# First expert layer: weights loaded as whole rows of 128 channels, the sums of the contraction kept open in six banks of PSUM

## The chip, the cores and the metric

The kernel runs as one program on one core of one Trainium2 chip. The metric is device microseconds (us) from the start of the program to its end. Three runs of the kernel before gave 3406.78, 3413.11 and 3400.99 us; their median is 3406.78 us.

Five engines work side by side, each on its own list of instructions: TensorE (PE; its loading of weights is shown apart, as PEld), VectorE (DVE), ScalarE (ACT), GpSimd (POOL) and SyncE (SP). SP issues nearly all loads of weights from HBM; 16 DMA engines carry them out. PSUM is the memory into which TensorE writes; it has eight banks of 512 fp32 per partition.

## The reference, cut to what matters

Two models are applied to 512 tokens of 1024 channels, all in fp32. The change touches one part of the first model: its mixture of eight experts, two for each token.

```python
def swiglu(h, w1, w3, w2):
    return (jax.nn.silu(h @ w1) * (h @ w3)) @ w2

def moe_swiglu(h, router_w, router_b, w1, w3, w2):
    logits = (h @ router_w).astype(jnp.float32) + router_b.astype(jnp.float32)
    top_logit, top_idx = lax.top_k(logits, TOP_K)
    top_p = jax.nn.softmax(top_logit, axis=-1)
    ...
    for e in range(N_EXPERTS):
        y = y + gates[..., e:e + 1] * swiglu(h, w1[e], w3[e], w2[e])
    return y
```

For each expert w1 and w3 are 1024 x 1408 and w2 is 1408 x 1024: 17.3 MB of fp32 from HBM for one expert.

## The kernel before, in words

`experts()` computes the layer. The tokens of each expert are counted on the chip; a tree of branches (`choose`) picks a body by the count: one unit is 64 tokens, and there are bodies for 1, 2, 2.25, 2.5, 3 and 4 units. In the profiled execution nine bodies run, in this order: expert 0 with 2 units; experts 1 and 2 with 144 and 160 tokens; expert 3 with 4 units, and the rest of its tokens in a body of 144; experts 4 and 5 with 1 unit; expert 6 with 144 tokens; expert 7 with 1 unit. They stand in the trace from about 1690 to 2385 us. Since each body is code of its own behind a branch, every engine takes branches between two bodies.

There are three kinds of body.

- **Whole** (2.25 and 2.5 units, `whole_weights`): the weight is the stationary operand, 128 x 128 at a time, and 144 or 160 tokens move. The sums stand with channels on the partitions, so the result has to be transposed (L648) before `row_out` (L564, on DVE) scales it.
- **Pieces** (2, 3 and 4 units, in `body`): tokens are stationary, the weight's columns move. For fp32 precision each loaded weight is split into a high and a low part (`split_into`: ACT L77, then DVE L80), and each product is three matmuls (`mm3`, L86, L89, L90).
- **Narrow** (1 unit): high and low parts of 64 tokens lie side by side, so a product with w1 or w3 takes two matmuls (L548 with the weight's high part, L549 with its low part); the product with w2 (`narrow_out`) uses the unsplit weight (L662).

In all three, w1 and w3 are taken in four chunks of their 1408 columns (`widths`: 384, 384, 384, 256). For a chunk, w1 and then w3 are loaded, each in two loads of 512 rows (`w_in`: 128 partitions x 4 row blocks x 384 columns, 768 KB, so pieces of 1536 contiguous bytes; 1024 bytes in the last chunk). The contraction of 1024 is summed at once for one chunk, in one PSUM tile ("up", four buffers), which is evacuated before the next chunk. w2 is taken in four quarters of 256 columns (`w_out`, two loads each, pieces of 1024 bytes); a narrow body takes it in two halves of 512 (pieces of 2048 bytes, L662). That is 24 loads for a body.

A load goes into one of two `raw` buffers of the body's parity (L495) or, three of five, one of three `wraw` buffers (L61), so five are in flight. SP waits at a load until the work on the buffer's last content is done. `nxt()` (the transposes of the next expert's tokens) stands ahead of the last chunk. Expert 7's narrow body adds its results to the output at once (`LastRows`, `take`, L1143 and L1147).

Of the kernel before, what the change touches and what calls it, by code (L numbers as in the profile page):

```python
# [10 lines left out]
F32 = mybir.dt.float32  # L11
# [9 lines left out]
KB = 8  # L21
# [10 lines left out]
class K:  # L32
# [37 lines left out]
    def split_into(self, parts, raw, step=None, eng=None, later=False):  # L70
        nc = self.nc
        hi, lo = parts
        n = raw.shape[1]
        step = step or n
        for i in range(0, n, step):
            c = slice(i, i + step)
# [388 lines left out]
def experts(k, ctx, tag, E, NF, xrows, yrows, dst, src, cnt, w1, w3, w2, variants, most, least=0, sums=None):  # L465
# [10 lines left out]
    n = -(-NFB // 3)  # L476
    widths = [128 * (NFB // n + (i < NFB % n)) for i in range(n)]
    WD = max(widths)
    FH = -(-NFB // 2)
# [19 lines left out]
    def parts(src, shape):  # L499
# [4 lines left out]
        return k.split_into(out, raw, 1 if i == 0 else None)  # L504
# [52 lines left out]
    def w_out(e, c, get):  # L557
        return [get(w2[e][f0 * 128:min(f0 + FH, NFB) * 128, c].rearrange("(fb p) n -> p fb n", p=128),
                    [128, min(FH, NFB - f0), c.stop - c.start]) for f0 in range(0, NFB, FH)]
# [29 lines left out]
    class LastRows:  # L589


        def __init__(self):
            self.now, self.left = {}, None

        def __call__(self, i, c):
            name, bufs = ("silu", 3) if i else (f"gu{c.start // 256 % 2}", 1)
            self.now[i] = hp.tile([128, WD], F32, name=name, bufs=bufs)[:, :256]
            return self.now[i]

        def done(self, q, c, sizes):  # L600
# [3 lines left out]
            self.left = lambda: sums.take(q, c, ys, lambda: pg.tile([128, 2, 256], F32, name="up", bufs=4))  # L604
# [6 lines left out]
    def whole_weights(e, b0, N, rx, nxt):  # L611
# [3 lines left out]
        c0 = 0  # L615
        for ci, n in enumerate(widths):
            f0, nf = c0 // 128, n // 128
            ps = []
            for w in (w1, w3):
                ws = w_in(w, e, c0, n, load)  # L620
                p = pg.tile([128, WD // 128, N], F32, name="up", bufs=4)[:, :nf]
                for f in range(nf):
                    for kb in range(KB):
                        nc.tensor.matmul(p[:, f], lhsT=ws[kb // 4][:, kb % 4, f * 128:(f + 1) * 128], rhs=xf[:, kb, 0:N],  # L624
                                         start=kb == 0, stop=kb == KB - 1)
                ps.append(p)
            h = hid[:, f0:f0 + nf]
            nc.scalar.activation(h, ps[0], AF.Silu)
            nc.vector.tensor_tensor(out=h, in0=h, in1=ps[1], op=OP.mult)  # L629
            c0 += n  # L630
            if ci == len(widths) - 2:
                nxt()
        sizes = [min(128, N - i) for i in range(0, N, 128)]
        ys = results(e, b0, rx)
        for q in range(4):
# [16 lines left out]
    def narrow_out(e, h, ys, share):  # L652

        for m in range(2):
            ps = pg.tile([128, 256], F32, name="yo")
            for f0 in range(0, NFB, 3):
                n = min(3, NFB - f0)
                w = load(w2[e][f0 * 128:(f0 + n) * 128, m * 512:m * 512 + 512].rearrange("(fb p) n -> p fb n", p=128),
                         [128, n, 512])
                for f in range(n):  # L660
                    for j in range(2):
                        nc.tensor.matmul(ps[j * S:j * S + S], lhsT=h[:, f0 + f], rhs=w[:, f, j * 256:j * 256 + 256],  # L662
                                         start=f0 + f == 0, stop=f0 + f == NFB - 1)
            for j in range(2):
                q = 2 * m + j
                c = slice(q * 256, q * 256 + 256)
                row_out(ys(0, c)[0:S], ps[j * S:j * S + S], c, share, j == 0)
                ys.done(q, c, [S])

    def body(e, b0, units, rx, nxt):  # L670
# [13 lines left out]
        c0 = 0  # L684
        for ci, n in enumerate(widths):
            acts = []
            for i, w in enumerate((w1, w3)):
                ws = w_in(w, e, c0, n, parts)
                for (b, half), x, h in zip(pieces, xs, hs):
                    ps = pg.tile([128, WD], F32, name="up", bufs=4)[:, :n]  # L690
                    for kb in range(KB):
                        product(ps, x[:, kb], [m[:, kb % 4] for m in ws[kb // 4]], half, kb == 0, kb == KB - 1)
                    f0, nf = c0 // 128, n // 128
                    if half:
                        g = hp.tile([128, WD], F32, name=f"gu{i}", bufs=1)[:, :n]
                        if i == 0:
                            nc.scalar.activation(g, ps, AF.Copy)
                            acts.append(g)
                            continue
                        nc.vector.tensor_copy(out=g, in_=ps)  # L700
                        pt = [pg.tile([128, nf, S], F32, name="tp") for _ in range(2)]
                        for q, t in enumerate((acts.pop(0), g)):
                            for f in range(nf):
                                nc.tensor.matmul(pt[q][:, f], lhsT=t[:, f * 128:(f + 1) * 128], rhs=two, start=True,
                                                 stop=True)
                        if units == 1:
                            a = h[:, f0:f0 + nf]
                        else:
                            a = hp.tile([128, WD // 128, S], F32, name="silu", bufs=3)[:, :nf]
                        nc.scalar.activation(a, pt[0], AF.Silu)  # L710
                        nc.vector.tensor_tensor(out=a, in0=a, in1=pt[1], op=OP.mult)
                        if units == 1:
                            continue
                    else:
                        if i == 0:
                            s = hp.tile([128, WD], F32, name="silu", bufs=3)[:, :n]
                            nc.scalar.activation(s, ps, AF.Silu)
                            acts.append(s)
                            continue
                        s = acts.pop(0)  # L720
                        nc.vector.tensor_tensor(out=s, in0=s, in1=ps, op=OP.mult)
# [6 lines left out]
            c0 += n  # L728
            if ci == len(widths) - 2:
                nxt()  # L730
        ys = results(e, b0, rx)
        if units == 1:
            narrow_out(e, hs[0], ys, sums and rx[3][:, 0:1])
            return
# [1905 lines left out]
```

## Time and profile before

| | |
|---|---|
| median of three runs | 3406.78 us (3400.99 to 3413.11) |
| the profiled execution: time, span of its records | 3420.45 us, 3418.6 us |
| mean granted clock of TensorE | 0.895 |
| instructions in the trace | 46334 |
| PE, PEld, DVE, ACT, POOL busy, share of the span | 87%, 70%, 51%, 38%, 16% |
| the nine bodies of the expert layer | about 1690 to 2385 us of the span |

The mean shares hide that the stages have different limits. In the rows further down a stretch of time is a line: the busy time of each engine in it with the number of instructions, the TensorE clock that was granted (1.00 is full speed), and the busy share of the DMA engines. A stage whose PE is busy all the time is TensorE's; one in which PE waits and the DMA share is near 1 is the loads'.

### The profile page before, as it was taken

How to read it: one execution, taken by the hardware profiler on the slowest of the kernel's cores; microseconds unless marked ns; L12 is line 12 of the kernel's file. 1: busy time of each engine (PE TensorE's matmuls, PEld its weight loads, DVE VectorE, ACT ScalarE, POOL GpSimd, SP SyncE). 2: the span in 40 equal slices, each digit the busy share in tenths (PEclk: the TensorE clock that was granted, in tenths of full speed). 3: DMA queues.
4: the chain of work that ended last, by engine and by line, in shares of the span. 5: the costliest groups of instructions: out<-in, count | busy, mean ns of one | idle time of the engine just before them, and what ended most of it. 6: DMA issues, size and time to landing. Idle time of an engine off the chain costs nothing. (4 is left out here: it accounts for less than half of the span.)

```text
span 3418.6 us, 46334 instructions
## 1 busy us (share of the span) xinstructions
PE 2960.8 (87%) x18016; PEld 2386.8 (70%) x18016; DVE 1753.9 (51%) x2902; ACT 1294.8 (38%) x2158; POOL 546.1 (16%) x701
## 2 busy tenths in 40 slices
PE   7989988899978499988678798787899969999996
PEld 3566977778767377867678798686676657666663
DVE  2544447775676755446340141604535547656565
ACT  2354433444433321123341241513353535555453
POOL 0011033333242300001400000202210021000001
PEclk8987978998979699999599899998999979999998
DMA  5455533332454455534487657988320149999995
GB/s 194 150 176 183 161 92 106 89 98 74 115 154 131 138 173 182 157 117 130 151 252 219 214 180 227 334 268 278 86 76 13 74 142 412 387 367 375 366 352 195
DMA packets 401120, 648.58 MB, mean 190 GB/s; under 512 B 94174, under 2 KB 300856, under 8 KB 375191
## 3 DMA queue, kind: packets, MB, share of 16 engines
q1 hardware_dynamic: 343290, 529.04, 46.2%
q10 hardware_dynamic: 40558, 56.91, 5.5%
q0 software_dynamic: 16944, 58.55, 5.1%
q8 instruction: 171, 2.80, 0.4%
q14 instruction: 157, 1.29, 0.1%
HBM read 584.81 MB, written 64.33 MB: 190 GB/s over the span
## 5 line engine op out<-in xcount | busy, mean ns | idle before, releaser
L80 DVE TENSOR_TENSOR wlo<-wraw,whi 128x1024 fp32r<-128x1024 f32 (+4 forms) x230 | 378.1, 1652 | 189.7 <-ACT whi L77 188.9
L77 ACT ACTIVATE whi<-wraw 128x1024 fp32r<-128x1024 f32 (+4 forms) x238 | 316.4, 1341 | 410.5 <-PE up L89 202.6
L80 DVE TENSOR_TENSOR wlo<-raw,whi 128x2048 fp32r<-128x2048 f32 (+3 forms) x102 | 205.8, 2020 | 72.0 <-ACT whi L77 71.8
L897 PE MATMUL up<-wlo,xx 128*128 128x512 f32 x512 | 225.0, 440 | 9.4 <-DVE wlo L80 8.9
L897 PE MATMUL up<-whi,xx 128*128 128x512 f32 x512 | 221.0, 432 | 9.9 <-ACT whi L77 8.5
L77 ACT ACTIVATE whi<-raw 128x2048 fp32r<-128x2048 f32 (+4 forms) x114 | 181.5, 1602 | 78.7 <-DMA raw<-in_rk_w_o_dram 25.4
L897 PEld LDWEIGHTS up<-wlo,xx 128*128 128x128 f32 x512 | 104.9, 205 | 78.7 <-issue 28.4
L90 PE MATMUL up<-hhi,wlo 128*128 128x512 f32 x352 | 142.4, 405 | 5.5 <-DVE wlo L80 5.4
L86 PE MATMUL up<-hhi,whi 128*128 128x512 f32 x352 | 142.0, 404 | 4.2 <-DVE hhi L212 4.1
L911 PEld LDWEIGHTS tu<-two,gu 128*128 128x128 f32 x512 | 124.5, 326 | 29.9 <-DVE gu L903 16.5
L89 PE MATMUL up<-hlo,whi 128*128 128x512 f32 x352 | 141.4, 402 | 0.0
L911 PE MATMUL tu<-two,gu 128*128 128x64 f32 x512 | 126.9, 391 | 12.6 <-DVE gu L903 10.5
L2062 POOL TENSOR_TENSOR tb<-Nb,Xb 128x60 f32<-128x60 f32 (+36 forms) x186 | 82.7, 444 | 315.8 <-DMA Nb<-ldram 302.0
L897 PEld LDWEIGHTS up<-whi,xx 128*128 128x128 f32 x512 | 105.8, 207 | 35.3 <-ACT whi L77 14.9
L2023 PE MATMUL pre<-AR,BKm 128*128 128x128 f32 (+1 forms) x768 | 120.5, 308 | 11.3 <-ACT BKm L2020 11.1
L927 PE MATMUL yo<-w2raw,hid 128*64 128x512 f32 x512 | 126.5, 617 | 0.9 <-DVE hid L914 0.9
L624 PE MATMUL up<-xf,raw 128*128 128x144 f32 (+1 forms) x640 | 92.5, 302 | 38.9 <-issue 37.8
L629 DVE TENSOR_TENSOR hs<-hs,up 128x432 f32<-128x432 f32 (+3 forms) x16 | 9.2, 578 | 218.6 <-PE up L624 218.6
L2023 PEld LDWEIGHTS pre<-AR,BKm 128*128 128x128 f32 x768 | 107.1, 216 | 14.8 <-ACT BKm L2020 11.6
L624 PEld LDWEIGHTS up<-xf,raw 128*128 128x128 f32 x640 | 88.4, 201 | 40.1 <-issue 38.8
L2168 DVE SCALAR_TENSOR_TENSOR S<-chain,wc,Sw 64x64 f32<-64x64 f32 x320 | 90.3, 282 | 45.7 <-ACT Y L2158 37.1
L2025 DVE TENSOR_TENSOR G<-pre,mask 128x512 f32<-128x512 f32 (+1 forms) x96 | 57.6, 601 | 99.7 <-PE pre L2023 98.7
(640 smaller groups left out, 7341.2 us busy)
## 6 DMA issues: line engine op xcount, KB each, us to landing
w2raw<-in_expert_w_down_dram SPq DMA_DIRECT2D x64, 1024.0 KB
raw<-in_moe_w_dram SPq DMA_DIRECT2D x75, 768.0 KB
wraw<-in_moe_w_dram SPq DMA_DIRECT2D x75, 768.0 KB
wraw<-in_ffn_w_dram SPq DMA_DIRECT2D x74, 512.0 KB
wraw<-in_ada_w_dram SPq DMA_DIRECT2D x72, 512.0 KB
wraw<-in_expert_w_gate_dram SPq DMA_DIRECT2D x33, 1024.0 KB
raw<-in_expert_w_up_dram SPq DMA_DIRECT2D x32, 1024.0 KB
wraw<-in_expert_w_up_dram SPq DMA_DIRECT2D x32, 1024.0 KB
```

Source lines behind the costliest of these rows:

```text
L77: t = nc.scalar.activation(hi[:, c], raw[:, c], AF.Copy)
L80: (eng or nc.vector).tensor_tensor(out=lo[:, c], in0=raw[:, c], in1=hi[:, c].bitcast(F32), op=OP.subtract)
L86: t = nc.tensor.matmul(ps, lhsT=l[0], rhs=r[0], start=start, stop=False)
L89: nc.tensor.matmul(ps, lhsT=l[0], rhs=r[1], start=False, stop=False)
L90: nc.tensor.matmul(ps, lhsT=l[1], rhs=r[0], start=False, stop=stop)
L624: nc.tensor.matmul(p[:, f], lhsT=ws[kb // 4][:, kb % 4, f * 128:(f + 1) * 128], rhs=xf[:, kb, 0:N], start=kb == 0, stop=kb == KB - 1)
L897: nc.tensor.matmul(ps, lhsT=l, rhs=s[m][:, q], start=kb == 0 and m == 0, stop=kb == KB - 1 and m == 1)
L911: nc.tensor.matmul(ps[:, i, f], lhsT=g[:, f], rhs=two, start=True, stop=True)
L927: nc.tensor.matmul(ps[i * S:i * S + S], lhsT=h[:, f], rhs=raws[f // 2][:, f % 2, i * 512:i * 512 + 512], start=f == 0, stop=f == NFB - 1)
L2023: nc.tensor.matmul(ps[:, i], lhsT=bkm[:, h, i].rearrange("p a t -> p (a t)"), rhs=AR[:, b, i].rearrange("p a t -> p (a t)")[:, :n2], start ...
L2062: eng.tensor_tensor(out=t, in0=N[:, rows, j:j + 1].to_broadcast([128, nr, ncl]), in1=X[:, j:j + 1, cols].to_broadcast([128, nr, ncl]), op= ...
L2168: nc.vector.scalar_tensor_tensor(out=o, in0=pn[r, h * C:h * C + C], scalar=w, in1=Sw[r, h * C:h * C + C], op0=OP.mult, op1=OP.add)
```

## The change

Each load is a block of 128 whole rows: `rows()` fetches 128 x 1408 of w1 or w3 (704 KB, 5632 contiguous bytes for a partition) or 128 x 1024 of w2 (512 KB, 4096 bytes). A body has 27 loads: eight of w1, eight of w3, eleven of w2. The contraction is the outermost loop: each block of 128 rows is multiplied into all columns before the next block comes, and the sums of all columns stay open in PSUM, in up to six "up" banks (`up_psum`), besides two "tp" banks; the "yo" tile is gone. Columns are taken as 512, 512, 384 (`banks`) or three 128-blocks to a bank (`threes`), and w2's as two of 512. All of w1 comes first, then all of w3, then all of w2; activations are made when a matrix is finished, and the results leave PSUM after the body's last matmul. `nxt()` stands after the fifth of w3's eight blocks.

```diff
-    def w_in(w, e, c0, n, get):
-        return [get(w[e][j * 512:(j + 1) * 512, c0:c0 + n].rearrange("(kb p) f -> p kb f", p=128), [128, 4, n])
-                for j in range(2)]
...
+    def rows(w, e, b, get):
+
+        return get(w[e][b * 128:(b + 1) * 128], [128, w[e].shape[1]])
+
+    def up_psum():
+        return pg.tile([128, 512], F32, name="up", bufs=6)
...
@@ whole_weights
+        for i, w in enumerate((w1, w3)):
+            ps = by_three(len(threes))
+            for kb in range(KB):
+                wt = rows(w, e, kb, load)
+                for f in range(NFB):
+                    nc.tensor.matmul(ps[f // 3][:, f % 3], lhsT=wt[:, f * 128:(f + 1) * 128], rhs=xf[:, kb, 0:N],
...
+                if i and kb == KB - 4:
+                    nxt()
...
+        ps = by_three(3)
+        for fb in range(NFB):
+            wt = rows(w2, e, fb, load)
+            for j in range(8):
+                nc.tensor.matmul(ps[j // 3][:, j % 3], lhsT=wt[:, j * 128:(j + 1) * 128], rhs=hid[:, fb],
...
         for q in range(4):
             c = slice(q * 256, q * 256 + 256)
-            ws = w_out(e, c, load)
-            ps = pg.tile([128, 2, N], F32, name="yo")
+            t = hp.tile([128, 320], F32, name="t", bufs=2)[:, :2 * N].rearrange("p (a b) -> p a b", a=2)
             for j in range(2):
-                for fb in range(NFB):
-                    nc.tensor.matmul(ps[:, j], lhsT=ws[fb // FH][:, fb % FH, j * 128:(j + 1) * 128], rhs=hid[:, fb],
-                                     start=fb == 0, stop=fb == NFB - 1)
-            t = hp.tile([128, 2, N], F32, name="silu", bufs=3)
-            nc.scalar.activation(t, ps, AF.Copy)
+                nc.scalar.activation(t[:, j], ps[(2 * q + j) // 3][:, (2 * q + j) % 3], AF.Copy)
             for i, r in enumerate(sizes):
                 pt = pg.tile([r, 2, 128], F32, name="tp")
@@ narrow_out
+        ps = up_psum()
+        for fb in range(NFB):
+            w = rows(w2, e, fb, load)
             for j in range(2):
...
+                nc.tensor.matmul(ps[j * S:j * S + S], lhsT=h[:, fb], rhs=w[:, j * 512:j * 512 + 512], start=fb == 0,
+                                 stop=fb == NFB - 1)
@@ body
+        for i, w in enumerate((w1, w3)):
+            ps = {(b, m): up_psum() for b, half in pieces for m in range(len(banks))}
+            for kb in range(KB):
+                ws = rows(w, e, kb, parts)
+                for (b, half), x in zip(pieces, xs):
+                    for m, (c0, c1) in enumerate(banks):
+                        product(ps[b, m][:, :c1 - c0], x[:, kb], [t[:, c0:c1] for t in ws], half, kb == 0, kb == KB - 1)
```

Two places show how the instructions move. The first is TensorE's list at the end of a whole body of 144 tokens (`hs` is the hidden layer, `silu` and `t` the copies of the sums that are transposed into `tp`, `raw` and `wraw` the loaded weights). Before, the last quarters read:

```order
L641 MATMUL yo<-hs,wraw 128x144 x17
L648 MATMUL tp<-ident,silu 128x128 x2
L648 MATMUL tp<-ident,silu 16x128 x2
L641 MATMUL yo<-hs,wraw 128x144 x7
L641 MATMUL yo<-hs,raw_14891 128x144 x6
```

Now:

```order
L637 MATMUL up<-hs,wraw 128x144 x24
L637 MATMUL up<-hs,raw_14735 128x144 x8
L637 MATMUL up<-hs,raw_14745 128x144 x8
L647 MATMUL tp<-ident,t 128x128
L647 MATMUL tp<-ident,t 16x128
L647 MATMUL tp<-ident,t 128x128
L647 MATMUL tp<-ident,t 16x128
L647 MATMUL tp<-ident,t 128x128 x2
L647 MATMUL tp<-ident,t 16x128 x2
L647 MATMUL tp<-ident,t 128x128 x2
L647 MATMUL tp<-ident,t 16x128 x2
```

Of the four groups of transposes three stood among the matmuls; now all four stand behind the last one, ahead of the body's end.

The second place is SP's list of loads in a narrow body, from the last chunk of w1 and w3 on. Before:

```order
L495 DMA raw_13760<-in_moe_w_dram 128x4x384
L495 DMA raw_13766<-in_moe_w_dram 128x4x384
L61 DMA wraw<-in_moe_w_dram 128x4x256 x3
L495 DMA raw_13874<-in_moe_w_dram 128x4x256
L495 DMA raw_13908<-in_moe_w_dram 128x3x512
L61 DMA wraw<-in_moe_w_dram 128x3x512 x2
L61 DMA wraw<-in_moe_w_dram 128x2x512
```

Now, from the last five blocks of w3 on:

```order
L494 DMA raw_13730<-in_moe_w_dram 128x1408
L494 DMA raw_13742<-in_moe_w_dram 128x1408
L61 DMA wraw<-in_moe_w_dram 128x1408 x3
L494 DMA raw_13826<-in_moe_w_dram 128x1408
L494 DMA raw_13860<-in_moe_w_dram 128x1024
L61 DMA wraw<-in_moe_w_dram 128x1024 x3
L494 DMA raw_13876<-in_moe_w_dram 128x1024
```

The turn of the buffers is the same (two `raw`, three `wraw`); a buffer holds one block of whole rows, and a load of w2 is 512 KB where most were 768 KB.

## Rows read from the trace of the kernel before

**Rows 1.** The page, busy time, share of the span and instructions of each engine.

```profile
PE 2960.8 (87%) x18016; PEld 2386.8 (70%) x18016; DVE 1753.9 (51%) x2902; ACT 1294.8 (38%) x2158; POOL 546.1 (16%) x701
```

**Rows 2.** Windows: start, end, length, busy time of each engine, PEclk, DMA share, GB/s.

```profile
1690.00:1760.80 70.80, 58.11 (x367) 54.87 (x367) 44.44 (x42) 48.20 (x72) 3.90 (x5) 0.89 0.80 258
...
1771.00:1841.80 70.80, 70.12 (x560) 69.51 (x560) 5.06 (x11) 9.33 (x24) 3.97 (x5) 0.98 0.72 230
1841.80:1855.40 13.60, 0.03 (x1) 0.06 (x1) 0.66 (x2) 0.00 (x0) 2.72 (x2) 0.65 0.77 218
...
1952.30:2055.50 103.20, 100.42 (x702) 100.03 (x702) 48.08 (x48) 47.69 (x71) 9.31 (x9) 0.97 0.62 194
2055.50:2125.40 69.90, 67.42 (x544) 66.39 (x544) 5.03 (x11) 3.65 (x9) 2.57 (x2) 1.00 0.71 223
...
2131.50:2180.20 48.70, 42.34 (x276) 34.97 (x276) 25.90 (x24) 26.83 (x42) 8.74 (x6) 0.95 0.95 327
...
2187.10:2236.40 49.30, 43.80 (x276) 35.42 (x276) 29.88 (x32) 27.07 (x38) 9.43 (x5) 0.93 0.94 323
...
2325.10:2384.90 59.80, 54.12 (x292) 44.60 (x292) 35.56 (x59) 20.91 (x22) 10.80 (x8) 0.84 0.93 314
```

**Rows 3.** PE's waits in 1690:2385: us in total, times, longest.

```profile
PE up L624 <- issue: 37.8, 4, 13.6
...
PE up L89 <- DVE wlo L80: 2.7, 2, 1.4
...
PE yo L86 <- ACT hs L725: 2.4, 1, 2.4
...
PE up L624 <- DMA raw<-in_moe_w_dram: 1.1, 1, 1.1
...
PE yo L641 <- DMA wraw<-in_moe_w_dram: 0.8, 1, 0.8
```

**Rows 4.** Queue q1 (packets, MB, share) in 1736:1747, 2136:2149, 2164:2175, 2900:3150.

```profile
q1 hardware_dynamic: 3823, 3.83, 107.8%
...
q1 hardware_dynamic: 2832, 4.22, 90.2%
...
q1 hardware_dynamic: 2147, 4.22, 102.6%
...
q1 hardware_dynamic: 11960, 87.10, 89.1%
```

**Rows 5.** Timeline of SP's loads around expert 4's end (start, us).

```profile
2169.69 1.94 SPq L61 DMA_DIRECT2D wraw<-in_moe_w_dram  x2
2177.70 0.93 SPq L495 DMA_DIRECT2D raw<-in_moe_w_dram  x2
```

**Rows 6.** Windows of full-clock matmuls of 384, 256 and 512 columns.

```profile
1975.00:1985.00 10.00, 9.92 (x57) 9.62 (x56) 0.00 (x0) 0.98 (x2) 1.00 0.51 159
...
2032.00:2050.00 18.00, 17.59 (x156) 17.41 (x155) 2.42 (x5) 0.00 (x0) 1.00 0.65 214
...
2471.00:2491.00 20.00, 20.00 (x90) 16.57 (x89) 0.00 (x0) 1.80 (x3) 1.00 0.45 153
```

**Rows 7.** Timeline of PE at the end of expert 1's body.

```profile
1841.12 0.66 PE L648 MATMUL tp<-ident,silu 128*128 128x128 f32 x4 [0.56 <-ACT silu L644]
1855.37 0.87 PE L624 MATMUL up<-xf,raw 128*128 128x160 f32 x2 [13.60 <-issue]
```

**Rows 8.** Groups of instructions in 1690:2400: busy us, mean ns, idle before.

```profile
L80 DVE TENSOR_TENSOR wlo<-raw,whi 128x1536 fp32r<-128x1536 f32 x25 | 43.8, 1754 | 13.9 <-ACT whi L77 13.7
...
L77 ACT ACTIVATE whi<-raw 128x1536 fp32r<-128x1536 f32 x25 | 37.0, 1484 | 21.6 <-DMA raw<-in_moe_w_dram 12.8 <-PE up L90 8.7
...
L564 DVE SCALAR_TENSOR_TENSOR x<-tp,share,gate 128x256 f32<-128x256 f32 x16 | 7.7, 484 | 86.4 <-PE tp L648 86.4
...
L1147 DVE SCALAR_TENSOR_TENSOR x<-up,x 128x256 f32<-128x256 f32 x16 | 6.2, 422 | 3.6 <-PE up L1143 3.2
...
L564 DVE SCALAR_TENSOR_TENSOR x<-tp,share,gate 16x256 f32<-16x256 f32 x12 | 5.6, 463 | 0.0
```

More of the change, by code (lines that the diff above doesn't have):

```diff
@@ L475, in experts @@
     S = 64
[L476 to L479, printed above, removed]
+    banks = [(c, min(c + 512, NF)) for c in range(0, NF, 512)]
+    threes = [(f, min(3, NFB - f)) for f in range(0, NFB, 3)]
     ahead = sums is not None
@@ L603, in done @@
                 self.left()
-            self.left = lambda: sums.take(q, c, ys, lambda: pg.tile([128, 2, 256], F32, name="up", bufs=4))
+            self.left = lambda: sums.take(q, c, ys, lambda: up_psum().rearrange("p (a b) -> p a b", a=2))
             if q == 3:
@@ L614, in whole_weights @@
         hid = hp.tile([128, NFB, N], F32, name="hs")
[L615 to L632, printed above, removed]
+        by_three = lambda n: [up_psum()[:, :3 * N].rearrange("p (a b) -> p a b", a=3) for _ in range(n)]
@@ L652, in narrow_out @@
     def narrow_out(e, h, ys, share):
[L654 to L663, printed above, removed]
-            for j in range(2):
[L665 to L668, printed above, removed]
+        ps = up_psum()
+        for fb in range(NFB):
+            w = rows(w2, e, fb, load)
+            for j in range(2):
+                nc.tensor.matmul(ps[j * S:j * S + S], lhsT=h[:, fb], rhs=w[:, j * 512:j * 512 + 512], start=fb == 0,
+                                 stop=fb == NFB - 1)
+        for q in range(4):
+            c = slice(q * 256, q * 256 + 256)
+            j = q // 2 * S
+            row_out(ys(0, c)[0:S], ps[j:j + S, q % 2 * 256:q % 2 * 256 + 256], c, share, q % 2 == 0)
+            ys.done(q, c, [S])
     def body(e, b0, units, rx, nxt):
@@ L683, in body @@
             hs.append(hp.tile([128, NFB, S] if units == 1 else [128, NFB, 2, n], F32 if units == 1 else F32R, name="hs"))
[L684 to L693, printed above, removed]
+        acts = {}
@@ new lines, in body @@
+        for i, w in enumerate((w1, w3)):
[5 more added lines that the diff above has]
+                        product(ps[b, m][:, :c1 - c0], x[:, kb], [t[:, c0:c1] for t in ws], half, kb == 0, kb == KB - 1)
+                if i and kb == KB - 4:
+                    nxt()
+            for (b, half), h in zip(pieces, hs):
+                if half or i == 0:
+                    acts[b] = hp.tile([128, NF], F32, name=f"act{i if units == 1 else b}", bufs=1)
+                for m, (c0, c1) in enumerate(banks):
+                    p, s = ps[b, m][:, :c1 - c0], acts[b][:, c0:c1]
+                    f0, nf = c0 // 128, (c1 - c0) // 128
@@ L706, in body @@
[L706 to L711, printed above, removed]
+                            nc.scalar.activation(s, p, AF.Copy)
+                        else:
+                            nc.vector.tensor_copy(out=s, in_=p)
@@ new lines, in body @@
+                        pt = pg.tile([128, nf, S], F32, name="tp")
+                        for f in range(nf):
+                            nc.tensor.matmul(pt[:, f], lhsT=s[:, f * 128:(f + 1) * 128], rhs=two, start=True, stop=True)
+                        wide = h if units == 1 else rx[1].rearrange("p a b -> p (a b)")[:, :NFB * S].rearrange(
+                            "p (f s) -> p f s", s=S)
+                        a = wide[:, f0:f0 + nf]
+                        if i == 0:
+                            nc.scalar.activation(a, pt, AF.Silu)
+                            continue
```

62 lines of the change are left out of this document (29 added, 33 removed).

## The prediction

> **What bounds the kernel now.** I read the page's busy times first: TensorE is busy for 87% of the span [rows 1]. That is a mean over stages, so I cut out the stage that the change touches. It lasts from 1690 to 2385 us, 695 us or a fifth of the span; nothing outside it changes. The windows by body [rows 2] show three kinds. The body of expert 1 (144 tokens, 1771.0 to 1841.8) has PE busy 70.1 of 70.8 us with the DMA engines at 0.72: TensorE sets its time, and so in the body with 4 units (100.4 of 103.2, share 0.62) and in the rest's (67.4 of 69.9, clock 1.00). The narrow bodies of experts 4 and 5 have PE busy 42.3 of 48.7 and 43.8 of 49.3 us, and DMA shares of 0.95 and 0.94: loads set their time. So they do for expert 7 (0.93), where the clock is only 0.84. Expert 0's lies between (PE 58.1 of 70.8, share 0.80). Between two bodies PE stands still, 13.6 us after expert 1. The table of waits calls that "issue": 37.8 us in four waits ahead of the whole bodies [rows 3]. No load or engine ends them; they belong to the branches and stay.
>
> So three questions decide: how much faster whole rows come in, for the bodies that loads set; what the matmuls' new shapes cost, for those that TensorE sets; and what stands uncovered at a body's end, now that the evacuation waits for the last matmul.
>
> **Run length of the loads.** Four windows in which little but one kind of load runs give the rate of the weight queue while it is busy: megabytes over share times window [rows 4]. Pieces of 1024 bytes: 3.83 MB / (1.078 x 11 us) = 323 GB/s. 1536 bytes: 4.22 / (0.902 x 13) = 360. 2048 bytes: 4.22 / (1.026 x 11) = 374. The last window is another layer's, with 8192 bytes: 87.10 / (0.891 x 250) = 391. The new pieces of 5632 and 4096 bytes lie between the last two. With a fixed time per piece and one per byte through these two I estimate 388 and 385 GB/s.
>
> A narrow body moves 9.44 MB in pieces of 1536 bytes, 2.10 MB in 1024 and 5.77 MB in 2048: 26.2 + 6.5 + 15.4 = 48.1 us, near its 48.7 and 49.3, as a body set by loads must. Afterwards: 11.53 MB / 388 + 5.77 / 385 = 29.7 + 15.0 = 44.7 us. That is -3.4 us each, **-10** for experts 4, 5 and 7. If both kinds came at 374, it were 46.3 (-1.8 each); at 391, 44.3 (-3.8). PE's busy 42 to 44 us lies just below, so more than 6 us each can't come.
>
> For expert 0, whose w2 comes in pieces of 1024 bytes, the sum is 50.6 us before and 44.7 after, -5.9. Its DMA share is 0.80, so loads set part of it only; I take **-4**, between 0 and -5.9.
>
> Loads get smaller as well: 704 and 512 KB in place of 768, 27 for 24. The row: with five in flight the queue was at 103% of 16 engines with loads of 768 and 512 KB [rows 4], so a load's fixed time is hidden by its neighbours. The Trainium skill, "DMA: Bandwidth & Descriptors", section "Measured (HBM→SBUF, 128 partitions, SWDGE, issued from GpSimd)", speaks against the change: it wants loads of at least 1 MiB, and 1 MB alone reaches 341 GB/s there. If the fixed time counted, three more loads in a body would cost; the trace does not agree, since smaller loads already came at 374 GB/s. SP's issue of a load is about 1 us for a pair [rows 5], 27 of them far below 45 us.
>
> **The end of a body's queue.** At expert 4's end SP issues the last pair at 2169.69 to 2171.63 and the next body's first load at 2177.70 [rows 5]: 6.1 us of branches in which only what is in flight can run. Before, the last five loads were 512, 768, 768, 768 and 512 KB, 3.4 MB; now they are five of 512 KB, 2.6 MB. The 0.8 MB less run dry 2 us earlier, at 380 GB/s. It counts only where a body set by loads follows another: expert 5 after 4. **+2** (0 to 4). Into a whole body it is hidden by PE's own branches and the loads' slack (share 0.72).
>
> **Shapes on TensorE.** At full clock 57 matmuls of 384 columns fill 10.0 us, 0.175 each; 156 of 256 columns take 17.6 to 18.0, 0.115; 90 of 512 columns 20.0, 0.222 [rows 6]. For 1408 columns that is 3 x 0.175 + 0.115 = 0.641 before and 2 x 0.222 + 0.175 = 0.620 now, 3% less; for w2's 1024 columns 0.461 and 0.444. In the body with 4 units, 96 sets of the first and 66 of the second: 2.0 + 1.1 = 3.1 us. I take **-2**, since its six banks are all refilled at once between w1, w3 and w2, where the splits of the next load (1.48 us on ACT, 1.75 on DVE [rows 8]) can stand ahead of an evacuation; that gives 0 to -3. Whole bodies keep their 128 x 128 x 144 matmuls: nothing but the order changes, 0.
>
> **Waits that go.** Whole bodies wait for loads twice in all, 1.1 us in a product with w1 or w3 and 0.8 us in one with w2 [rows 3]; a chunk needs two loads of 768 KB before its sums can end, a block of whole rows one of 704 KB. **-2** (0 to -2). Expert 0 also waits 2.4 us for its hidden layer ahead of w2 [rows 3]; the first of w2's products again needs the evacuation, so that stays, inside the -4 above.
>
> **The tails.** In a whole body the last group of transposes, 0.66 us for four, starts 0.56 us after the last matmul [rows 7], so PE ends 1.2 us after it. The three other groups stood among the matmuls, 2.0 us. Now all four come last, in two "tp" buffers that DVE empties by `row_out`, 0.484 and 0.463 us [rows 8]. Transposes of the last quarter wait for the sixth of eight: about 0.4 for a first copy, 0.3 for transposes, 6 x 0.474 = 2.8 and the last pair 0.3: 3.9 us. That is 2.7 more, less 2.0 saved: **+3** for four whole bodies. If the branches behind overlap it, 0; if PE's transposes do not get cheaper by being gathered, +11.
>
> Expert 7's four takes now all stand behind the last matmul: two of them, 8 matmuls and four additions of 0.422 us [rows 8] each, were among w2's. Two takes more are 3.4 us on DVE: **+3.5** (2 to 4).
>
> **Sum:** -10 - 4 + 2 - 2 - 2 + 3 + 3.5 = -9.5 us. Against the profiled execution's 3420.45 us that gives 3411; the median of the runs is 13.7 us lower, 3406.8, so **3397 us** for the median. That is 0.28%; about 0.3% (10 us) is what a measurement here can tell from no change. All lower bounds together give 3386 us, all upper ones 3420; since they don't fall together, the forecast's own range is 3389 to 3408.
>
> **Rivals.**
>
> - *Loads stop being the bound.* If whole rows, which lie in one piece in HBM, come faster than any row shows, each body falls to PE's busy time [rows 2]: -6.4, -5.5 and -5.7 us for 4, 5 and 7 and -12.7 for expert 0, with the other terms -28: 3379 us. Against it: the four rates flatten off towards 391.
> - *Slower: TensorE starves between loads and its clock falls.* With the contraction outermost, PE in a narrow body gets one block of 128 rows at a time: 2 x 0.62 = 1.24 us of matmuls per 1.86 us of transfer. At half clock (1.2 GHz) it is 2.48 us, and PE becomes the bound: 16 x 0.62 = 10 us for a body, 30 for three, and the 10 us of gain are lost as well; in half of the loads that is +15 and about 5 lost: 3417 us, in all of them 3437. It decides where the mean clock of w1 and w3 falls below 1.24 / 1.86 = 0.67. For it: expert 7's 0.84 [rows 2]. Against it: before, a load brought four row blocks, 1.40 us of matmuls per 2.18 us of transfer, 64% against 67% now, and the clock was 0.95 and 0.93. The Trainium skill, "TensorE: Matmul & The Clock Gate", section "HAM oscillation — how this bites in real kernels", warns of just such a loop, and advises to finish the contraction of a tile first. By that rule the time is this rival's; the trace bears it out in expert 7 alone.
> - *Given back.* Rates stay at 374 GB/s (-5.4 for three bodies), expert 0 gains 2, the 4 units nothing, the tails cost 8, expert 7 4, the dry queue 2, and the waits for loads (2) go: together about +5: 3412 us.
>
> **How the numbers follow.** Forecast 0.52, loads no longer the bound 0.14, clock 0.14, given back 0.20. The forecast lies on the border of what counts as faster (3396.6), so half of it, and the first rival: faster 0.40. The other half and most of the last rival: same 0.41. The clock and the worst tails: slower 0.19. The range takes in the first rival and what is given back, 3379 to 3415; the clock rival and some of the rest stay outside.
>
> **What would show it.** Right: windows of experts 4 and 5 some 3 us shorter at a DMA share still above 0.9 and rates of 385 GB/s; matmuls of 512 columns at 0.222 us; about 4 us between the last w2 matmul and the last transpose of a whole body; SP's gap between bodies unchanged. Wrong: a clock below 0.8 in the narrow bodies; PE waits for "up" banks in the body of 4 units; longer "issue" waits between bodies, which I hold unchanged; weight-queue rates no better than 374.

## The result, and the profile after

The change made the kernel slower: the ratio of the changed kernel to the one before is 1.0083 (95% interval 1.0055 to 1.0110), that is 19 to 37 us. The median of five runs is 3436.99 us beside 3407.06 for the kernel before.

The busy times of the changed kernel's page hardly differ from [rows 1]:

```profile
PE 2964.6 (86%) x17446; PEld 2336.0 (68%) x17446; DVE 1759.1 (51%) x2891; ACT 1296.4 (38%) x2163; POOL 553.6 (16%) x701
```

The windows of the changed kernel by body answer to [rows 2]: expert 0, expert 1, the body with 4 units, the rest's, and experts 4, 5 and 7. (Expert 0's window starts here at its first product; in [rows 2] it starts some 10 us ahead of it.)

```profile
1692.20:1751.00 58.80, 55.75 (x237) 45.03 (x237) 42.49 (x38) 41.59 (x51) 0.00 (x0) 0.90 0.72 250
1762.30:1834.40 72.10, 70.68 (x560) 69.27 (x560) 5.03 (x11) 9.66 (x28) 3.96 (x5) 0.98 0.68 228
...
1944.90:2047.20 102.30, 100.48 (x467) 83.66 (x468) 49.01 (x47) 44.78 (x61) 4.32 (x7) 0.98 0.55 190
2049.60:2118.30 68.70, 67.33 (x544) 65.93 (x544) 4.96 (x11) 4.99 (x16) 3.10 (x3) 1.00 0.76 240
2125.60:2180.00 54.40, 45.81 (x200) 28.76 (x200) 28.95 (x27) 25.39 (x39) 15.05 (x6) 0.92 0.79 287
2186.80:2242.60 55.80, 47.42 (x200) 30.62 (x200) 28.93 (x28) 26.71 (x36) 9.55 (x5) 0.86 0.78 282
2332.40:2396.30 63.90, 54.74 (x216) 33.85 (x216) 36.61 (x59) 19.33 (x19) 12.43 (x8) 0.90 0.85 303
```

The narrow bodies, which should have become shorter, are 4 to 6 us longer each (54.4, 55.8 and 63.9 against 48.7, 49.3 and 59.8). Their DMA share fell from 0.93 to 0.95 down to 0.78 to 0.85: the loads did not become the lighter bound, they stood still for longer. Cut in two, the bodies of experts 4 and 5 show where. First the kernel before:

```profile
2131.50:2156.50 25.00, 20.60 (x105) 18.80 (x105) 16.41 (x13) 13.71 (x14) 8.74 (x6) 0.91 1.02 348
2156.50:2180.20 23.70, 21.74 (x171) 16.17 (x171) 9.49 (x12) 13.12 (x29) 0.00 (x0) 1.00 0.88 304
2187.10:2212.10 25.00, 21.48 (x101) 18.48 (x102) 19.87 (x21) 14.46 (x13) 9.43 (x5) 0.86 1.01 349
2212.10:2236.40 24.30, 22.33 (x177) 16.94 (x175) 10.01 (x12) 12.60 (x25) 0.00 (x0) 1.00 0.86 297
```

And the changed one:

```profile
2125.60:2150.60 25.00, 23.02 (x92) 17.80 (x93) 19.93 (x18) 14.96 (x16) 15.05 (x6) 0.83 0.89 326
2150.60:2180.00 29.40, 22.79 (x109) 10.96 (x108) 9.03 (x10) 10.42 (x23) 0.00 (x0) 1.00 0.71 253
2186.80:2211.80 25.00, 21.16 (x88) 15.70 (x88) 17.92 (x16) 15.34 (x15) 9.55 (x5) 0.89 0.98 363
2211.80:2242.60 30.80, 26.26 (x112) 14.92 (x112) 11.01 (x12) 11.37 (x22) 0.00 (x0) 0.83 0.61 217
```

The second part is 5.7 and 6.5 us longer, at DMA shares of 0.71 and 0.61 in place of 0.88 and 0.86.

The weight queue alone, over the whole bodies of experts 4 and 5 (packets, MB, share). First the kernel before:

```profile
q1 hardware_dynamic: 9304, 14.19, 83.3%
...
q1 hardware_dynamic: 9576, 14.59, 85.4%
```

And the changed one:

```profile
q1 hardware_dynamic: 3234, 14.04, 70.2%
...
q1 hardware_dynamic: 3297, 14.32, 70.0%
```

Share times window is, as an estimate, the time in which the queue was busy: 40.6 and 42.1 us before, 38.2 and 39.1 us now, 2.4 and 3.0 us less. The time in which it was dry went from 8.1 and 7.2 us to 16.2 and 16.7 us.

Within expert 4's second part ten microseconds tell most. DMA by slices (40 slices, so 0.25 us each; the digit is the busy share in tenths) and the weight queue, 2160 to 2170 us, changed kernel:

```profile
DMA  5411100000913999842000000000009317899888
...
q1 hardware_dynamic: 376, 1.34, 38.8%
```

The same window of the kernel before, also near the end of its narrow body:

```profile
DMA  9669586899999998999999999999999999999999
...
q1 hardware_dynamic: 1859, 3.45, 97.3%
```

After the change the queue runs dry twice, 1.34 MB come in place of 3.45. SP's timeline says why (start, time from the first issue to the end of the last, count of loads):

```profile
2151.82 6.00 SPq L61 DMA_DIRECT2D wraw<-in_moe_w_dram  x3
2161.56 5.45 SPq L494 DMA_DIRECT2D raw<-in_moe_w_dram  x2
2167.51 2.04 SPq L61 DMA_DIRECT2D wraw<-in_moe_w_dram  x3
```

Four of the first five loads of w2 are issued by 2157.8. The fifth is issued at 2161.56, the sixth by 2167.0 (the end of that pair). Between them stand ACT and DVE. ACT (L540 are the sixteen activations of the next expert's tokens):

```profile
2154.44 1.38 ACT L77 ACTIVATE whi<-wraw 128x1408 fp32r<-128x1408 f32 x1 [1.23 <-DMA wraw<-in_moe_w_dram]
2155.72 2.89 ACT L540 ACTIVATE xf<-tp,fsh,fsc 128x128 f32<-128x128 f32 x8
2158.46 1.42 ACT L77 ACTIVATE whi<-raw 128x1408 fp32r<-128x1408 f32 x1
2159.73 2.94 ACT L540 ACTIVATE xf<-tp,fsh,fsc 128x128 f32<-128x128 f32 x8
```

DVE:

```profile
2159.91 1.62 DVE L80 TENSOR_TENSOR wlo<-raw,whi 128x1408 fp32r<-128x1408 f32 x1 [2.43 <-ACT whi L77]
2162.13 1.75 DVE L699 COPY act<-up 128x512 f32<-128x512 f32 x3 [0.59 <-PE up L548]
...
2165.64 0.35 DVE L710 TENSOR_TENSOR hs<-hs,tp 128x192 f32<-128x192 f32 x1 [0.25 <-PE tp L702]
```

PE:

```profile
2161.59 0.91 PE L548 MATMUL up<-wlo,xx 128*128 128x512 f32 x3 [0.75 <-DVE wlo L80]
2162.96 2.64 PE L702 MATMUL tp<-two,act 128*128 128x64 f32 x22 [0.47 <-ACT xx L77]
2165.53 1.08 PE L657 MATMUL up<-raw,hs 128*64 128x512 f32 x4
...
2172.72 1.08 PE L657 MATMUL up<-wraw,hs 128*64 128x512 f32 x4 [1.38 <-DMA wraw<-in_moe_w_dram]
```

So the chain at the seam between w3 and w2 is: eight activations delay the high part of w3's last block (2158.46); DVE's low part ends at 2161.53, and only this frees a buffer (2161.56); PE's last product with w3 ends at 2162.5; three copies, 22 transposing matmul instructions and three multiplications make the hidden layer (complete at 2166.0); w2's first block is used, and with that its buffer is free (2166.6). Until then five buffers hold all of w2 that can be loaded, 2.6 of 5.8 MB. The other six blocks come late, and PE waits for them.

The table of PE's waits, 1690 to 2397 us, answers to [rows 3]:

```profile
PE up L620 <- issue: 35.8, 3, 13.6
...
PE up L548 <- DVE wlo L80: 9.5, 15, 0.8
PE up L657 <- DMA wraw<-in_moe_w_dram: 5.5, 7, 1.4
...
PE up L86 <- ACT hs L721: 2.7, 3, 1.7
...
PE up L657 <- DMA raw<-in_moe_w_dram: 2.5, 5, 1.1
```

The whole bodies' waits for loads are gone. For w2's blocks in narrow bodies PE waits 8.0 us (L657), where the kernel before waited 2.6 us:

```profile
PE yo L662 <- DMA raw<-in_moe_w_dram: 2.1, 3, 0.9
...
PE yo L662 <- DMA wraw<-in_moe_w_dram: 0.5, 2, 0.4
```

### The profile page after: what moved, and what is told of

Same layout as the page of the kernel before. It is cut to its first block, busy times and chain, and to the rows that moved or that the text cites. A ratio compares the mean times of both kernels' runs of the same rounds, so it can differ in the third digit from the quotient of the medians.

```text
span 3430.9 us, 45254 instructions
## 1 busy us (share of the span) xinstructions
PE 2964.6 (86%) x17446; PEld 2336.0 (68%) x17446; DVE 1759.1 (51%) x2891; ACT 1296.4 (38%) x2163; POOL 553.6 (16%) x701
## 5 line engine op out<-in xcount | busy, mean ns | idle before, releaser
L80 DVE TENSOR_TENSOR wlo<-wraw,whi 128x1024 fp32r<-128x1024 f32 (+3 forms) x230 | 375.3, 1642 | 199.9 <-ACT whi L77 190.3
L77 ACT ACTIVATE whi<-wraw 128x1024 fp32r<-128x1024 f32 (+3 forms) x238 | 314.0, 1334 | 409.4 <-PE up L89 209.9
L80 DVE TENSOR_TENSOR wlo<-raw,whi 128x2048 fp32r<-128x2048 f32 (+2 forms) x106 | 209.5, 1980 | 96.9 <-ACT whi L77 96.8
L77 ACT ACTIVATE whi<-raw 128x2048 fp32r<-128x2048 f32 (+3 forms) x118 | 184.1, 1572 | 85.2 <-DMA raw<-in_rk_w_o_dram 24.8
L620 PE MATMUL up<-xf,raw 128*128 128x144 f32 (+1 forms) x616 | 85.2, 300 | 37.2 <-issue 35.8
L620 PEld LDWEIGHTS up<-xf,raw 128*128 128x128 f32 x616 | 83.0, 199 | 39.1 <-issue 39.1
L461 POOL DMA_INDIRECT xres<-x,l_at x13 | 28.3, 2173 | 489.1 <-DVE x L562 384.6
```

What stands on the lines that cost most here:

```text
L620: nc.tensor.matmul(ps[f // 3][:, f % 3], lhsT=wt[:, f * 128:(f + 1) * 128], rhs=xf[:, kb, 0:N], start=kb == 0 and f % 3 == 0, stop=kb == K ...
```

## The experiments

All times of bodies are taken between PE's idle stretches of over 4.5 us, in one profile each; the layer runs from expert 0's first product to the mixer behind. "Ratio" is to the kernel before, over several executions; a profile is one of them, and not always a typical one (that of `both` took 3409.98 us, the shortest of its six, which go up to 3455.98). "w1w3", "w2" and "take" divide the sum of the three narrow bodies by PE's instructions: up to the end of the last product with w1 or w3 (L548 and L549 before, L547 and L548 after), from there to the end of the last product with w2 (L662 before, L657 after), and expert 7's takes behind it.

```
                    e4    e5    e7    sum     w1w3    w2  take layer  ratio (95% interval)
before             48.8  49.3  59.7  157.8   114.1  39.4   4.3  702.0
before_copy        48.6  50.5  57.8  156.9   114.3  38.3   4.3  700.9  1.0014 (0.9995 to 1.0034)
changed            54.4  55.8  63.9  174.1   112.1  54.2   7.8  721.4  1.0083 (1.0055 to 1.0110)
after_again        51.8  53.3  65.7  170.8   109.9  53.1   7.8  718.1
no_hidden_wait     48.8  52.7  56.1  157.6   113.8  36.0   7.8  710.1
two_more           56.0  58.8  60.5  175.3   114.8  52.7   7.8  721.4  1.0079 (1.0048 to 1.0110)
prep_in_w2         50.4  50.2  64.1  164.7   103.2  53.7   7.8  713.2  1.0053 (1.0025 to 1.0082)
both               49.6  54.5  60.1  164.1   110.2  46.1   7.8  712.1  1.0106 (1.0064 to 1.0149)
seven              50.7  54.5  57.9  163.1   111.4  43.9   7.8  705.0  1.0065 (1.0040 to 1.0090)
seven_prep         52.0  47.8  57.3  157.1   105.0  44.3   7.8  704.7  1.0036 (1.0008 to 1.0065)
best               49.9  47.9  56.9  154.7   103.3  43.6   7.8  699.6  1.0055 (1.0028 to 1.0082)
short_runs         54.4  57.9  63.1  175.3   112.1  55.4   7.8  722.7
four               58.7  55.5  66.0  180.2   116.8  55.6   7.8  721.7
filler             52.3  54.5  64.4  171.3   107.0  56.5   7.8  722.8
```

**before_copy and after_again**, no edit.

> The kernel before, word for word, as a second sample: its ratio to itself should be 1.000 within 0.3%, its stretch of the expert layer 702 us within 4, the bodies of experts 4, 5 and 7 at 48.8, 49.3 and 59.7 within 1.5. If the stretch differs by more than 5 us, differences of a few us between single profiles carry nothing.

> The changed kernel, word for word, as a second profile: the stretch of the expert layer 721 us within 4, experts 4 and 5 at 54.4 and 55.8 us within 1.5.

The kernel before, measured against itself, is the same within its interval, and its layer within 1.1 us. The changed kernel's layer is 721.4 and 718.1: 18 us longer than 701.5. Of that, 15 us are the three narrow bodies (172.4 against 157.4). A single body differs by up to 2.6 us from one profile to the next, beyond the 1.5 expected, so the experiments are read by the sum of the three, whose two values lie within 3.3 us.

The three parts repeat better and show the place: the stretch of w2 took 39.4 and 38.3 us before and takes 54.2 and 53.1 us now, 15 us more; expert 7's takes went from 4.3 to 7.8 us; up to the last product with w3 the bodies are 3 us shorter. Before, w2's first products, on chunks already finished, start 2.5 us ahead of the last product with w1 or w3; now they start 3.0 to 5.2 us behind it.

**no_hidden_wait.**

```diff
-                nc.tensor.matmul(ps[j * S:j * S + S], lhsT=h[:, fb], rhs=w[:, j * 512:j * 512 + 512], start=fb == 0,
+                nc.tensor.matmul(ps[j * S:j * S + S], lhsT=h[:, fb % KB, 0:S], rhs=w[:, j * 512:j * 512 + 512], start=fb == 0,
...
-            narrow_out(e, hs[0], ys, sums and rx[3][:, 0:1])
+            narrow_out(e, rx[1], ys, sums and rx[3][:, 0:1])
```

> In narrow bodies w2's products take the body's input tokens in place of the hidden layer, so they need not wait for it (the values are then wrong, and with them what follows in the second model; only the bodies of experts 4, 5 and 7 are read). Theory A (the seam): in the changed kernel the queue runs dry for about 5 us between w3 and w2 because w2's buffers come free only when the hidden layer is made; without that wait expert 4's and 5's bodies fall from 54.4 and 55.8 us to 46 to 49, the DMA share rises from 0.79 to 0.9 or more. Theory B (contraction outermost starves PE block by block, and its clock): the waits lie inside w1 and w3, so the bodies stay at 53 us or more. Theory C (whole rows are not transferred faster): the DMA share rises but the bodies stay at 49 us or more.

Expert 4 and the sum (157.6, -14.8) are back at the kernel before; expert 5, at 52.7, missed its 46 to 49, and expert 4's DMA share came to 0.86, not 0.9. The gain lies in the stretch of w2 alone (36.0 us in place of 53.7): theory A names the place. But the edit takes away more than the change added, since the kernel before also had to wait for its hidden layer, so 14.8 us is no measure of what the seam alone costs.

**two_more, prep_in_w2 and both.**

```diff
+            if fb < 2:
+                w = hp.tile([128, 1024], F32, name=f"raw{1 - turn[1]}", bufs=2)
+                nc.sync.dma_start(out=w, in_=w2[e][fb * 128:(fb + 1) * 128])
...
-                if i and kb == KB - 4:
+                if units > 1 and i and kb == KB - 4:
...
+            if fb == 5:
+                nxt()
```

> The first two blocks of w2 of a narrow body go into the two buffers of the other parity, which are idle then: seven loads of 512 KB in flight at the seam in place of five, 1 MB more. Theory A: 1 MB at about 400 GB/s is 2.6 us of dry queue less in each narrow body, 8 us in all: expert 4 at 51 to 52.5 us, 3428 to 3431 for the median. Theories B and C: no change, 3437, expert 4 at 54.

> In narrow bodies the transposes of the next expert's tokens, with their sixteen activations on ACT, move from w3's fifth block to behind w2's sixth, where ACT is idle. Theory A: the split of w3's last block was delayed by eight of these activations, 2.3 us, so the hidden layer, and with it w2's buffers, come 2 to 3 us earlier: expert 4 at 51.5 to 52.5 us, 6 us less in all (expert 7 has none to move, so two bodies gain), 3431 to 3433 for the median. Theories B and C: within 1 us of the changed kernel in each body, 3437.

> Both edits: two more buffers for w2 and the transposes behind w2's sixth block. Theory A: the gains add, expert 4 and 5 at 49 to 50 us, near the kernel before (48.7 and 49.3), median 3423 to 3427. Theories B and C: 3437, no body more than 1 us shorter.

Two more buffers for w2 alone did not help (175.3): a miss. SP's timeline of this kernel at expert 5's start shows when they were issued:

```profile
2177.67 1.62 SPq L61 DMA_DIRECT2D wraw<-in_moe_w_dram  x3
2179.47 1.94 SPq L657 DMA_DIRECT2D raw<-in_moe_w_dram  x2
2184.47 2.71 SPq L494 DMA_DIRECT2D raw<-in_moe_w_dram  x2
```

The two loads of w2 (L657) were put right behind the body's first five, since their buffers were free: 1 MB ahead of w1's sixth block. The stretch of w2 got shorter in expert 7 alone (15.7 us; the changed kernel has 19.4 and 20.8). In experts 4 and 5 it took 18.7 and 18.2 us, where the changed kernel has 15.9 to 17.5; the granted clock in it was 0.82 and 0.81, so the experiment decides nothing on theory A. Moving the transposes behind w2's sixth block took 7.7 us off the sum, experts 4 and 5 down to 50.4 and 50.2, somewhat more than the 2 to 3 us expected for each. All of it lies ahead of the last product with w3 (103.2 us in place of 111.0), where the splits no longer stand behind the activations; the stretch of w2 stays as long (53.7). "both" carries the fault of the first edit: expert 4 is at 49.6, expert 5 at 54.5, and its median of 3448.99 us missed the 3423 to 3427.

**seven, four and seven_prep**: the same idea without that fault, since the buffers are used in turn. (`four` has `max(2, turn[2] - 3)` and 4 in place of 7, seven_prep the second edit from above as well.)

```diff
-        if i % 5 < 2:
-            raw = hp.tile(shape, F32, name=f"raw{turn[1]}", bufs=2)
+        j = i % turn[2]
+        if j < turn[2] - 3:
+            raw = hp.tile(shape, F32, name=f"raw{(turn[1] + j // 2) % 2}", bufs=2)
...
-        turn[:] = [0, e % 2]
+        turn[:] = [0, e % 2, 7 if units == 1 else 5]
```

> Narrow bodies also use the two load buffers of the other parity, in turn with the five: seven loads in flight in place of five, in w1 and w3 as well. Theory A2 (buffers held by the splits): w1 and w3 take 36 to 38 us in the changed kernel although their 11.5 MB at the 415 GB/s of undisturbed pieces need 28, because a buffer comes free only after its two splits on ACT and DVE, which stand in line behind evacuations and the next expert's activations; two more blocks in flight bring experts 4 and 5 from 54.4 and 55.8 us to 49 to 52. Rival B (TensorE, starved at the start and then at half clock): no change in w1 and w3, bodies at 54 or more. Rival C (the transfers themselves): DMA share stays as it is, no change.

> The changed kernel with four loads in flight in the narrow bodies in place of five. Theory A2 (a load can only be issued when a buffer's splits or products are done, so the number of buffers sets the narrow bodies): experts 4, 5 and 7 grow by 3 us or more each (5 to 7 buffers took 1 to 6 us off each). Rival B (TensorE and its clock) and rival C (the transfers): no change beyond 2 us.

> Seven loads in flight, and the next expert's transposes behind the sixth block of w2. Theory A2: the two gains add in part, experts 4 and 5 at 46 to 49 us, below the kernel before; median 3412 to 3420. Rivals B and C: as with the transposes moved alone, 50 to 51 us, 3421.

Four, five and seven loads in flight give a sum of 180.2, 172.4 and 163.1 us: the more buffers, the shorter the narrow bodies together. From five to seven the gain lies in the stretch of w2 (53.7 to 43.9 us), not in w1 and w3 (111.0 and 111.4), where the expectation had put it; from five to four most of the loss lies in w1 and w3. In single bodies the order doesn't hold everywhere: expert 5 is at 55.5 with four and 54.5 with seven, which missed its 49 to 52, and with four neither it nor expert 7 (66.0) grew by the 3 us expected. With the transposes moved as well the two gains add: the sum is 157.1, as before the change; not below it, and expert 4 at 52.0 missed its 46 to 49.

**short_runs**: pieces of 1408 and 1024 bytes in loads of the same size.

```diff
-        return get(w[e][b * 128:(b + 1) * 128], [128, w[e].shape[1]])
+        n = w[e].shape[1]
+        g, q = b // 4 % 2 * 512, b % 4 * (n // 4)
+        return get(w[e][g:g + 512, q:q + n // 4].rearrange("(a p) f -> p a f", p=128), [128, n])
```

> The changed kernel with every load of the same size into the same buffer, but read as four row groups by a quarter of the columns: pieces of 1408 bytes in place of 5632 and 1024 in place of 4096 (the weights then stand in wrong places, the last blocks of w2 are read twice from elsewhere, and the second model's routing is another; only the first layer's bodies are read). Theory A2 (release of buffers sets the narrow bodies): they grow by less than 2 us each, whole bodies not at all. Rival C (transfers set them): 17.3 MB at 350 instead of 410 GB/s is 7 us more for experts 4 and 5.

The weight queue of the changed kernel, 2196 to 2207 us (w1 and w3 of expert 5), and of this one, 2128 to 2140 us (of expert 4):

```profile
q1 hardware_dynamic: 697, 3.49, 77.8%
```

```profile
q1 hardware_dynamic: 2386, 3.26, 76.0%
```

As in [rows 4]: 3.49 / (0.778 x 11) = 408 GB/s with long pieces, 3.26 / (0.760 x 12) = 357 with short ones. Single windows mislead, though: 2188 to 2200 us of the changed kernel gives 3.63 MB / (0.858 x 12) = 353. Over the whole bodies of experts 4 and 5 the same working gives 345 to 351 GB/s for the kernel before (two profiles), 367 to 386 for the changed one (two profiles) and 332 and 338 for this one. So the long pieces are faster while they run; but without them the sum is 175.3, 3 us more than 172.4 and within what profiles differ in. Expert 4 is at 54.4 and expert 5 at 57.9, 1.3 and 3.3 us more than the changed kernel's means, so expert 5 missed its 2 us. Rival C, at 7 us more for each of the two, is out. The length of the pieces, for which whole rows were the means, is worth little here.

**filler**: more work for TensorE.

```diff
+                if idle is not None:
+                    for _ in range(2):
+                        nc.tensor.matmul(idle, lhsT=xs[0][:, kb].rearrange("p a s -> p (a s)"), rhs=ws[1][:, 0:512], start=True, stop=True)
```

> The changed kernel with two idle matmuls of 512 columns behind each of w1's eight blocks in narrow bodies; their sums are never read. They keep TensorE busier while it would wait for the next block. Rival B (starving lowers the granted clock, and that is what the narrow bodies lose): the clock of the first 25 us rises from 0.79 to 0.88 to above 0.95, and the bodies get shorter by 2 us or more though they do more. Theory A2: the clock may rise, but the bodies get no shorter than 54 and 56 us by more than 1 us.

Windows of the filler kernel, halves of experts 4 and 5:

```profile
2115.50:2140.50 25.00, 23.86 (x110) 19.63 (x110) 19.50 (x17) 14.18 (x15) 12.74 (x6) 0.93 0.84 317
2140.50:2167.90 27.40, 22.84 (x106) 12.42 (x106) 9.45 (x10) 10.89 (x24) 0.00 (x0) 0.94 0.72 262
2174.80:2199.80 25.00, 24.58 (x109) 20.17 (x110) 20.11 (x18) 17.66 (x19) 8.31 (x5) 0.88 0.99 374
2199.80:2229.30 29.50, 24.86 (x109) 12.81 (x107) 9.12 (x10) 9.61 (x19) 0.00 (x0) 0.88 0.63 229
```

The clock of the first 25 us is 0.93 and 0.88; it did not pass 0.95, so what a full clock would give stays open. What it shows is that sixteen more matmuls in w1 cost no time (sum 171.3). In expert 5, at nearly the same clock (0.88 beside 0.89), PE's busy time in the first 25 us rises from 21.16 to 24.58 us and the body is no longer than before (54.5 beside 55.8 and 53.3): TensorE isn't the bound there. The second parts stay about as long, at DMA shares of 0.72 and 0.63.

**best**: seven_prep, and two of the eight result transposes of a whole body in "up" banks.

```diff
-                pt = pg.tile([r, 2, 128], F32, name="tp")
+                if q:
+                    pt = pg.tile([r, 2, 128], F32, name="tp")
+                else:
+                    pt = up_psum()[:r, :256].rearrange("p (a b) -> p a b", a=2)
```

> As before it (seven loads, transposes behind w2's sixth block), and in whole bodies the first two of eight result transposes go into a free up bank in place of a tp bank. The tail after the last w2 matmul was 3.9 us, with 0.4 us waits on DVE; with two more banks it is 3.0 to 3.6 us, four bodies gain 0.3 to 0.9 us each, 1 to 3 us in all, less than the median can tell: read from the windows.

In PE's timeline the four groups of transposes at the end of experts 1 and 2 take 3.7 us in place of 4.0: a little gained, less than expected, and not to be seen in the bodies (72.2 and 79.0 us; 72.0 and 79.0 in the changed kernel). The narrow sum is lower than any other, 154.7 us, but within what profiles differ in from seven_prep's 157.1, which has the same narrow bodies; the layer is at 699.6, the ratio still 1.0055. No version beats the kernel before.

## Why the prediction was wrong, point by point

**The step that failed** is "Run length of the loads", and in it the sentence "near its 48.7 and 49.3, as a body set by loads must". From a high DMA share I took it that the transfers set the narrow bodies, and gave the whole gain in rate to their length: -10 us for three. Measured: +15, of which 3.5 are expert 7's takes, a term of its own; that leaves +11.6. The agreement of 48.1 with 48.7 us was chance: it puts 17.3 MB into the body, but in expert 4's window the weight queue moved 14.19 MB and was busy for 83.3% of it; the rest came ahead of the body's first product.

The rate did rise, from about 348 to about 374 GB/s over whole bodies, short of the 388 and 385 assumed, and the queue's busy time did fall, by 2.4 and 3.0 us in experts 4 and 5 where 3.4 was forecast. What the sum has no term for is the time in which the queue is dry: it grew by 8.1 and 9.5 us. A load must first be issued, and it is issued when a buffer is free. Before, the buffers held 768 KB, and w2's came while the last, narrow chunk of w3 was still to come; a chunk's evacuation was short, and near the body's end the queue stayed at 97%. Now a load of w2 is 512 KB, all of the hidden layer is made after the last block of w3, and eight of the next expert's sixteen activations stand ahead of that block's split.

Undoing one of these at a time moved the sum of 172.4 us down to 157.6 (no wait for the hidden layer), 164.7 (activations moved) and 163.1 (seven buffers); shortening the pieces again moved it by 3. That the loop order with its few buffers costs the time, and not the row length, is what these runs show; how much of it loads of 512 KB in place of 768 alone would cost was not tried. The mended kernels show what the loop order is worth without the line of activations: up to the last product with w3 they take 103 to 105 us, before 114; they lose it again in the stretch of w2 (44 beside 39) and in the takes.

**The end of a body's queue** (+2) saw the right thing, fewer bytes in flight and a dry queue, at the wrong place: I looked at the branches behind the body and not at the seam within it, where the same five buffers wait for a computation. What was missing is to ask, for each load, which instruction frees its buffer. The rival "given back" ended at 3412, too little for the same reason.

**Shapes on TensorE** (-2) was mis-sized. In the body with 4 units the changed kernel's matmuls of 512 columns, 2040 to 2047 us, run at full clock:

```profile
2040.00:2047.00 7.00, 7.00 (x32) 5.61 (x30) 1.70 (x5) 0.00 (x0) 1.00 0.98 393
```

In PE's timeline there they start 0.233 us apart, not 0.222 as read from [rows 6]. That 0.222 was itself a misreading: the 90 matmuls of the window take in those that only touch its ends, and in PE's timeline they start 0.227 us apart (2471.18, 2471.40, 2471.63). With 0.233, 1408 columns cost 2 x 0.233 + 0.175 = 0.641 us, just what they cost before, and w2's 1024 columns 0.466 against 0.461. That body and the rest's together take 173.4 and 172.8 us, against 173.1 and 171.3: no gain.

**The tails** (+3) were right. The end of expert 1's body in PE's timeline answers to [rows 7]:

```profile
1830.38 0.60 PE L647 MATMUL tp<-ident,t 128*128 128x128 f32 x4
1831.54 0.68 PE L647 MATMUL tp<-ident,t 128*128 128x128 f32 x4 [0.56 <-ACT t L643]
1832.62 0.67 PE L647 MATMUL tp<-ident,t 128*128 128x128 f32 x4 [0.40 <-ACT t L643]
1833.69 0.68 PE L647 MATMUL tp<-ident,t 128*128 128x128 f32 x4 [0.40 <-DVE x L562]
```

From 1830.4 to 1834.4 are 4.0 us, where I had 3.9 and the kernel before 1.2. Experts 1, 2 and 6 take 1.4, 0.7 and 0.2 us more (means of two profiles each), 0.7 each having been forecast. **Waits that go** (-2) were right too: no wait of a whole body for a load is left.

**Expert 0** (-4, between 0 and -5.9): 60.9 us became 58.7 and 59.0, -2. **Expert 7's takes** (+3.5) were right: from the end of the last product with w2 to the end of the body PE takes 7.8 us in both profiles of the changed kernel, 4.3 in both of the kernel before. **The branches** stayed: the stretches between bodies add up to 1.8 us more.

**The rival of the clock** isn't what happened in the main; that it gave 3437 us for all loads, the measured median, is chance. It needed a mean clock below 0.67 in w1 and w3; up to the last product with w3 the narrow bodies had 0.82 to 0.93. The clock of the bodies of experts 4 and 5 was 0.92 and 0.86 against 0.95 and 0.93 in the first profile, and 1.00 in the second part of both in after_again, which is 3 us longer than before all the same (26.8 and 28.3 us against 23.7 and 24.3, the rest of a body after its first 25 us). A part it may have: expert 5's second part took 30.8 us at a clock of 0.83 beside those 28.3, and in expert 7 the stretch of w2 took 19.4 and 20.8 us at 0.82 and 0.78, before 14.0 at 1.00 twice. How much of that the clock costs no run here separates.

The Trainium skill ("TensorE: Matmul & The Clock Gate", section "HAM oscillation — how this bites in real kernels") advises to finish the contraction of a tile before waiting for loads, and gives the clock as the reason. For the kernel as changed the advice fits (172.4 us for the narrow bodies against 157.4), but the trace shows another reason for most of it. A finished chunk is evacuated, and w2's products with it begun, while loads go on.

**What stays open.** The layer explains 18 us of the 30 between the medians; the interval begins at 19. The rest of the program took 2716.6 and 2695.9 us in the two profiles of the kernel before, 2709.5 and 2704.5 in those of the changed one, so no difference can be read there. Nor is it known why the mended kernels, whose layer is about as short as before, stay 0.36 and 0.55% slower. Their executions scatter more: nine of seven_prep's twelve took 3398.62 to 3419.65 us and three 3437.62 to 3445.79, at a mean clock of 0.886 to 0.891 beside 0.897 to 0.903, while the kernel before kept to 3394.68 to 3419.57 in the same series. The profiles of the two mended kernels are of executions of 3410.91 and 3416.85 us, so where the long ones lose their time can't be read.

## What to carry to other kernels

A DMA share near 1 says that the engines were fed, not that faster transfers shorten the stage: set the bytes that the queue moved within the window against those that the stage needs, and ask of each buffer which instruction frees it, and what that instruction waits for. Where one matrix's result feeds the next, loads ahead must cover the whole evacuation between them; a loop order that gathers the evacuation at the end needs that many more bytes in flight. Before a contraction is put outermost, look at what it gathers (sums to evacuate, activations of other work) and whether the splits that free the buffers stand in the same line.

## What the runs showed of the hardware that was not expected

The rate of one kind of load depends on the window of some 11 us in which it is read: pieces of 5632 bytes came at 408 GB/s in one (2196 to 2207 us), above the 391 of 8192-byte pieces in another layer [rows 4], and at 353 in the one before it. Matmuls of 512 columns at full clock ran every 0.233 us in one layer and 0.227 in another. The rest of one and the same program differed by 21 us between two executions, which is more than the 18 us that the layer lost.
